# Two unused stretches in the shared SBUF pool: operands of TensorE at multiples of 256 bytes

## The chip, the cores and the metric

The kernel runs on one core of one Trainium2 chip. The metric is the time of one execution on the device in microseconds (us). The figures here come from three timed runs, and from one further execution that the hardware profiler recorded (the trace).

## The reference: what is computed

The program is a small decoder trunk on a sequence of 256 tokens with 1024 channels, in float32. It has two layers, and each layer is a half-step feed-forward block (FFN), a token mixer, and a second half-step FFN. The first layer mixes with Mamba-2, the second with sliding-window attention to a shared K and V. Every sub-layer normalises its input first. Cut to what matters:

```
def swiglu_half_step(h, g, w1, w3, w2):
    u = rmsnorm(h, g)
    return h + FFN_HALF * ((jax.nn.silu(u @ w1) * (u @ w3)) @ w2)

for layer in range(DEPTH):                       # DEPTH = 2
    h = swiglu_half_step(h, ffn_norm[layer, 0], ...)
    if layer < N_A_LAYERS:                       # layer 0
        h = h + mamba2_mixer(rmsnorm(h, ssm_norm[i]), ...)
    else:                                        # layer 1
        h = h + sliding_window_attention(rmsnorm(h, attn_norm[j]), k_shared, v_shared, ...)
    h = swiglu_half_step(h, ffn_norm[layer, 1], ...)
    if layer == N_A_LAYERS - 1:
        k_shared, v_shared = shared_kv(h, kv_norm, w_kv, k_norm)
return h
```

The four FFNs have 1024 x 2816 weights `w1` and `w3` and 2816 x 1024 weights `w2`; they hold most of the arithmetic.

## The kernel before

**Split operands.** TensorE multiplies in float32r. To keep float32 accuracy each operand is split into a high part and a low part, both float32r, and a product is the sum of three matmuls (`mm3` and `wmm3`, lines 135 to 145): high by high, high by low, low by high. All of them are issued by `mm` at line 111, so nearly every matmul of the profile stands under line 108, and one tells them apart by the names of their tiles.

**Weights.** A `Unit` (line 149) loads 1 MB of weights from HBM into `raw` over SP's DMA queue. ScalarE copies it to the high part `wh` (line 171), VectorE subtracts to get the low part `wl` (line 172). There are 8 buffers of each.

**The operands that are not weights.** In a feed-forward block, and in the projections of the mixers, they live in three places:

- `uT`, the normalised input, high and low, 16 KB for each partition in the pool `const` (line 90). `Norm.normalize` (line 294) writes it.
- `vh` and `vl`, the input times the gain but not yet normalised, tag `v` in the pool `sb` (`Norm.open`, line 252, and `Norm.split`, line 256). The first two chunks of each FFN (`c < 2`, line 356), the first gates of Mamba (`z_first`, line 653) and the queries (`q_mm`, line 953) use these, so that TensorE can begin before the statistics of the norm are known. Mamba borrows the same tag for `xdt` (line 676) and the last FFN for `rows` (line 423).
- `ghl`, the gated product of an FFN chunk, high and low halves side by side, tag `ghl` in `sb`, 4 buffers (line 345). Mamba's `yhl` (line 804) shares the tag.

**How an FFN goes.** `run_ffn` (line 306) runs over 11 chunks of 256 hidden columns. For each chunk, `up` multiplies by `w1` and `w3`, `gate` makes `ghl`, and `flush` multiplies the gated product of the chunk before by `w2` into four accumulators (`acc`). From chunk 2 on, `up_wide` (line 370) streams high and low parts of `uT` together, 512 columns at once, and then 256 columns for `wl`. The narrow form streams 256 columns at a time. In the last FFN, `down_t` (line 400) turns the roles round: `ghl` is the stationary operand, and 512 columns of weights stream past it. The queries (`pq`) do the same with `vh` and `vl`.

**Order of the work.** The planner of the tile framework puts the instructions of each engine in order and places the semaphores. It also places tiles: within a pool, tags lie one behind the other in the order in which the code first asks for them, each size rounded up to 32 bytes; a pool opened later lies behind. In the built kernel before the change the start addresses within each partition, with the remainder by 256, are:

| tile | first byte | remainder |
|---|---|---|
| `uT` (pool `const`) | 25,824 | 224 |
| `wh`, first of 8; `wl`, first of 8 | 67,136; 99,904 | 64 |
| tag `g` (first of the pool `sb`) | 132,672 | 64 |
| tag `v`: `vh`, `vl` | 135,744 and 143,936 | 64 |
| `rsb`, `cv` | 152,256; 154,304 | 192 |
| `ghl` / `yhl`, 4 of 2,048 bytes | 158,400 | 192 |
| `sq` | 166,592 | 192 |
| end of `sb`, start of `xp`, `mp`, `ap` | 171,584 | 64 |

Rows of `uT`, `vh`, `vl` and the two halves of `ghl` are 1,024 bytes apart, and the 128 weights that a matmul holds begin 512 bytes apart within `wh` and `wl`. Each of these tensors therefore has one remainder by 256 for all its matmuls.

Of the kernel before, what the change touches and what calls it, by code (L numbers as in the profile page):

```python
# [11 lines left out]
F32 = mybir.dt.float32  # L12
# [6 lines left out]
P = 128  # L19
# [21 lines left out]
def yoco_kernel(ctx: ExitStack, tc: tile.TileContext, a: dict, out: bass.AP):  # L41
# [7 lines left out]
    sb = ctx.enter_context(tc.tile_pool(name="sb", bufs=2))  # L49
# [15 lines left out]
    def x_part(b):  # L65
        nc.sync.dma_start(xin[:, :, b * 256:(b + 1) * 256], xsrc[:, :, b * 256:(b + 1) * 256])

    x_part(0)
    grow = [sb.tile([4 * KT, P], F32, tag="g", name="grow0", bufs=3),
            sb.tile([3 * KT, P], F32, tag="g", name="grow1", bufs=3)]  # L70
    nc.scalar.dma_start(grow[0], a["ffn_norm"].rearrange("l j (k p) -> (l j k) p", p=P))
# [133 lines left out]
    def keep_warm(n):  # L205
        pw = ps_mm.tile([P, P], F32, tag="mm", name=nm("pw"))
        for i in range(n):
            nc.tensor.matmul(pw, dummy, dummy, start=True, stop=True)
# [932 lines left out]

    n0 = norms[0]
    n0.open()
    w13 = a["ffn_w1"][0, 0], a["ffn_w3"][0, 0]
    keep_warm(10)
    ups = {0: [up_unit(*w13, 0, 0, 4, True, {1: lambda: x_part(1), 3: lambda: x_part(2)}),
# [98 lines left out]
```

## Time and profile before

| | |
|---|---|
| median of three runs | 1044.17 us (1042.39, 1044.17, 1044.38) |
| the profiled execution, own time | 1042.34 us |
| its span in the trace | 1040.6 us, 18036 instructions |
| TensorE (PE) busy | 1028.8 us, 99% of the span, 7160 matmuls |
| weight loads (PEld) | 944.6 us, 91% |
| VectorE (DVE) | 735.1 us, 71% |
| ScalarE (ACT) | 602.9 us, 58% |
| HBM read | 184.90 MB, 179 GB/s over the span |
| granted clock of TensorE | 1.00 |

How to read it: matmuls are pipelined, so the record of one (about 280 ns for 256 columns) overlaps the records of the next two or three. The record's length is therefore not the time that a matmul costs. What it costs in a stream is the distance from start to start (the pace), and that is read from the chain of waits, which gives for a piece of the chain its length and its number of matmuls: length divided by number is the pace.

### The profile page before, as it was taken

The numbers are of one execution on the slowest core, as the hardware profiler recorded it, in microseconds if no ns is written. First come the engines' busy times: TensorE is split into PE (matmuls) and PEld (weight loads), VectorE is DVE, ScalarE is ACT, GpSimd is POOL, SyncE is SP. The second block draws the span as 40 slices with busy tenths as digits, with TensorE's granted clock in tenths as the row PEclk, the third lists the DMA queues.
The fourth block names the chain that finished last, engine by engine and source line by source line (L and its number), as shares of the span: only waits on it lengthen the run. The fifth ranks groups of instructions, "written<-read, shape, count | busy, mean of one in ns | idle before, by whom it ended". The sixth has DMA issues, their size and how long they took to land.

```text
span 1040.6 us, 18036 instructions
## 1 busy us (share of the span) xinstructions
PE 1028.8 (99%) x7160; PEld 944.6 (91%) x7160; DVE 735.1 (71%) x1252; ACT 602.9 (58%) x1040; POOL 57.4 (6%) x78
## 2 busy tenths in 40 slices
PE   8899999999999999999999999999999999999998
PEld 8899999999999999999999999999996699888887
DVE  6866656789999988656556975665677678565653
ACT  6564545668976756455545754455567565455551
POOL 1100000003220010000000000100002000000000
PEclk9999999999999999999999999999999999999999
DMA  8676565658564365746465555594641436464641
GB/s 284 172 243 202 165 200 185 180 170 255 166 180 163 124 204 163 234 158 215 163 203 188 177 171 195 174 299 162 217 162 41 123 116 210 162 210 161 221 136 41
DMA packets 139589, 187.19 MB, mean 180 GB/s; under 512 B 5100, under 2 KB 122000, under 8 KB 139504
## 3 DMA queue, kind: packets, MB, share of 16 engines
q1 hardware_dynamic: 137168, 179.32, 52.8%
q0 software_dynamic: 2288, 6.69, 2.4%
q8 instruction: 56, 0.92, 0.4%
q14 instruction: 29, 0.24, 0.1%
q10 hardware_dynamic: 48, 0.02, 0.0%
HBM read 184.90 MB, written 1.11 MB: 179 GB/s over the span
## 4 chain that ended last, share of the span: by engine, by line
PE 91%; DVE 3%; DMA 3%; ACT 1%; SPq 1%; issue 0%; POOL 0%; DVEq 0%; ACTq 0%
PE pm L108 45%; PE acc L108 23%; PE pp L108 9%; PE pa L108 5%; DMA raw<-in_ffn_w_dram 2%; PE pq L106 2%; PE pa L106 1%; PE py L108 1%; DVE wl L172 1%; PE pz L108 1%; PE ps L106 1%; PE po L106 1%; DVE sp L997 1%; SPq L158 1%; PE pkv L108 1%; DMA raw<-in_ssm_w_in_dram 1%
## 5 line engine op out<-in xcount | busy, mean ns | idle before, releaser
L172 DVE TENSOR_TENSOR wl<-raw,wh 128x1024 fp32r<-128x1024 f32 (+1 forms) x372 | 412.2, 1130 | 87.3 <-ACT wh L171 86.9
L171 ACT CAST wh<-raw 128x1024 fp32r<-128x1024 f32 (+1 forms) x372 | 347.5, 970 | 110.5 <-PE acc L108 43.6
L108 PE MATMUL pm<-uT,wh 128*128 128x512 f32 (+1 forms) x1216 | 403.9, 381 | 1.7 <-DVE tp L330 1.6
L108 PE MATMUL pm<-uT,wl 128*128 128x256 f32 x1152 | 321.5, 280 | 0.0
L108 PEld LDWEIGHTS pm<-uT,wh 128*128 128x128 f32 x1216 | 223.6, 188 | 45.3 <-DVE tp L330 2.4
L108 PEld LDWEIGHTS pm<-uT,wl 128*128 128x128 f32 x1152 | 216.6, 188 | 1.0
L108 PE MATMUL acc<-ghl,wh 128*128 128x256 f32 x1056 | 190.6, 281 | 0.6 <-ACT ghl L347 0.6
L339 ACT COPY lo<-pm 128x256 f32<-128x256 f32 x136 | 50.3, 370 | 198.0 <-PE pm L108 198.0
L108 PEld LDWEIGHTS acc<-ghl,wh 128*128 128x128 f32 x1056 | 162.2, 188 | 2.9 <-ACT ghl L347 0.9
L340 DVE TENSOR_TENSOR tp<-pm,lo 128x256 f32<-128x256 f32 x136 | 57.5, 423 | 129.5 <-ACT lo L339 129.4
L108 PE MATMUL acc<-ghl,wl 128*128 128x256 f32 x528 | 148.5, 282 | 0.0
L108 PE MATMUL pp<-uT,wh 128*128 128x256 f32 x576 | 104.8, 283 | 0.1
L108 PEld LDWEIGHTS acc<-ghl,wl 128*128 128x128 f32 x528 | 99.4, 188 | 0.0
L108 PEld LDWEIGHTS pp<-uT,wh 128*128 128x128 f32 x576 | 88.8, 189 | 0.7 <-DVE uT L304 0.3
L108 PE MATMUL pp<-uT,wl 128*128 128x256 f32 x288 | 80.7, 281 | 0.0
L108 PE MATMUL pm<-vh,wh 128*128 128x256 f32 x256 | 73.3, 287 | 1.3 <-ACT wh L171 1.3
L108 PE MATMUL pm<-vh,wl 128*128 128x256 f32 x256 | 72.4, 284 | 0.5 <-DVE wl L172 0.5
L108 PE MATMUL pm<-vl,wh 128*128 128x256 f32 x256 | 72.3, 283 | 0.0
L108 PE MATMUL acc<-wh,ghl 128*128 128x512 f32 x176 | 58.3, 395 | 0.0
L108 PEld LDWEIGHTS pp<-uT,wl 128*128 128x128 f32 x288 | 54.3, 188 | 0.0
L347 ACT CAST ghl<-g 128x256 fp32r<-128x256 f32 x88 | 35.5, 403 | 31.7 <-DVE g L344 31.4
L108 PEld LDWEIGHTS pm<-vh,wh 128*128 128x128 f32 x256 | 48.9, 191 | 1.4 <-ACT wh L171 1.4
(236 smaller groups left out, 1253.5 us busy)
## 6 DMA issues: line engine op xcount, KB each, us to landing
raw<-in_ffn_w_dram SPq DMA_DIRECT2D x168, 512.0 KB, 4.9
raw<-in_ffn_w_dram SPq DMA_DIRECT2D x44, 1024.0 KB, 5.4
raw<-in_ssm_w_in_dram SPq DMA_DIRECT2D x16, 1024.0 KB, 5.5
raw<-in_ssm_w_out_dram SPq DMA_DIRECT2D x8, 1024.0 KB, 5.3
raw<-in_ssm_w_in_dram SPq DMA_DIRECT2D x8, 512.0 KB, 5.1
pr<-pdram POOLq DMA_DIRECT2D x8, 512.0 KB, 4.6
raw<-in_w_q_dram SPq DMA_DIRECT2D x4, 1024.0 KB, 5.0
raw<-in_w_o_dram SPq DMA_DIRECT2D x4, 1024.0 KB, 5.1
```

Source lines behind the costliest of these rows:

```text
L106: r = op(*args, **kw)
L108: r = op(*args, **kw)
L158: nc.sync.dma_start(view(raw, shape, lo, n0)[:, k0:k0 + src.shape[1]], src)
L171: return (nc.scalar.copy(wh, rs).ins, nc.vector.tensor_sub(wl, rs, wh.bitcast(F32)).ins)
L172: nc.vector.tensor_sub(wl, rs, wh.bitcast(F32)).ins)
L339: nc.scalar.copy(lo, pw[:, 256:512])
L340: nc.vector.tensor_add(o, pw[:, 0:256], lo)
L347: nc.scalar.copy(gh, g)
L997: chain[1] = op(*args, **kw).ins
```

## The change

Two tiles that no instruction reads or writes are asked for in the pool `sb`. The first, 48 floats (192 bytes), is asked for ahead of the tag `g`; the second, 32 floats (128 bytes), behind the tag `v`.

```diff
@@ -66,6 +66,7 @@
     x_part(0)
+    sb.tile([P, 48], F32, tag="gap0", name="gap0", bufs=1)
     grow = [sb.tile([4 * KT, P], F32, tag="g", name="grow0", bufs=3),
             sb.tile([3 * KT, P], F32, tag="g", name="grow1", bufs=3)]
@@ -1141,6 +1142,7 @@
     n0 = norms[0]
     n0.open()
+    sb.tile([P, 32], F32, tag="gap1", name="gap1", bufs=1)
     w13 = a["ffn_w1"][0, 0], a["ffn_w3"][0, 0]
```

Added up from the sizes, `g` moves to 132,864 and `v` to 135,936 (both 192 bytes on); `rsb`, `cv`, `ghl` and `sq` move 320 bytes on, to 152,576, 154,624, 158,720 and 166,912. All of these are multiples of 256. What lies behind, the pools `xp`, `mp` and `ap`, moves by 320 bytes too and begins at 171,904 (remainder 128). `uT`, `raw`, `wh` and `wl` stay where they are. No instruction is added, removed or given another size.

## The prediction

> **What bounds the kernel now.** First the page: which engine is busy, and what the chain that ended last is made of.
>
> ```profile
> PE 1028.8 (99%) x7160; PEld 944.6 (91%) x7160; DVE 735.1 (71%) x1252; ACT 602.9 (58%) x1040; POOL 57.4 (6%) x78
> ...
> PEclk9999999999999999999999999999999999999999
> ...
> PE 91%; DVE 3%; DMA 3%; ACT 1%; SPq 1%; issue 0%; POOL 0%; DVEq 0%; ACTq 0%
> PE pm L108 45%; PE acc L108 23%; PE pp L108 9%; PE pa L108 5%; DMA raw<-in_ffn_w_dram 2%; PE pq L106 2%; PE pa L106 1%; PE py L108 1%; DVE wl L172 1%; PE pz L108 1%; PE ps L106 1%; PE po L106 1%; DVE sp L997 1%; SPq L158 1%; PE pkv L108 1%; DMA raw<-in_ssm_w_in_dram 1%
> ```
>
> TensorE is 91% of the chain, at full clock throughout. The only way for a move of tiles to reach the end is therefore the pace of the matmuls. The waits of PE say the same: the longest sums are small.
>
> ```profile
> PE pm L108 <- DVE tp L330: 1.6, 1, 1.6
> PE pm L108 <- ACT wh L171: 1.3, 1, 1.3
> ```
>
> Second, the groups by line and form, which give how many matmuls read a tensor that moves.
>
> ```profile
> L108 PE MATMUL acc<-ghl,wh 128*128 128x256 f32 x1056 | 190.6, 281 | 0.6 <-ACT ghl L347 0.6
> L108 PE MATMUL acc<-ghl,wl 128*128 128x256 f32 x528 | 148.5, 282 | 0.0
> L108 PE MATMUL pm<-vh,wh 128*128 128x256 f32 x256 | 73.3, 287 | 1.3 <-ACT wh L171 1.3
> L108 PE MATMUL pm<-vh,wl 128*128 128x256 f32 x256 | 72.4, 284 | 0.5 <-DVE wl L172 0.5
> L108 PE MATMUL pm<-vl,wh 128*128 128x256 f32 x256 | 72.3, 283 | 0.0
> L108 PE MATMUL acc<-wh,ghl 128*128 128x512 f32 x176 | 58.3, 395 | 0.0
> L108 PE MATMUL acc<-wl,ghl 128*128 128x512 f32 x88 | 34.6, 394 | 0.0
> L108 PE MATMUL pa<-yhl,wh 128*128 128x256 f32 x128 | 23.3, 284 | 0.0
> L108 PE MATMUL pa<-yhl,wl 128*128 128x256 f32 x64 | 18.0, 281 | 0.0
> L106 PE MATMUL pq<-wl,vh 128*128 128x512 f32 x32 | 12.5, 390 | 0.0
> L108 PE MATMUL pz<-vl,wh 128*128 128x256 f32 x32 | 9.0, 283 | 0.0
> ```
>
> So 1056 + 528 + 128 + 64 = 1776 matmuls stream 256 columns of the tag `ghl`. The tag `v` is streamed by 3 x 256 = 768 in the FFNs (192 in each) and by 3 x 32 = 96 in Mamba's first gates. With the roles turned, 176 + 88 = 264 matmuls hold `ghl` and 3 x 32 = 96 hold `v`, while 512 columns of weights stream.
>
> Third, the pace. These are pieces of the chain in order of time: start, length, what, how many.
>
> ```profile
> 282.90 16.38 PE pp L108 x138
> ...
> 388.16 7.20 PE pm L108 x60
> ...
> 398.89 7.18 PE pm L108 x60
> 406.07 2.85 PE acc L108 x24
> 408.93 5.75 PE pm L108 x48
> 414.68 5.70 PE acc L108 x48
> ...
> 759.02 8.54 PE acc L108 x72
> 767.56 9.56 PE pq L106 x42
> 838.59 11.26 PE pa L108 x96
> ...
> 876.29 5.58 PE acc L108 x24
> ```
>
> The `pm` pieces from 388 to 415 us are the first two chunks of an FFN, so they stream `v`. Their pace is 7.20/60 = 120.0, 7.18/60 = 119.7 and 5.75/48 = 119.8 ns. The 256-column `acc` pieces stream `ghl`: 5.70/48 = 118.75, 8.54/72 = 118.6 ns; I use 118.7. The `pa` piece streams `uT`: 11.26/96 = 117.3 ns. So does the `pp` piece, 16.38/138 = 118.7 ns. All have the same 256 columns, the same clock and weights with the same remainder, 64. The pace thus differs by up to 2.4 ns from tensor to tensor, but the one tensor `uT` also has two paces, so the remainder does not settle it alone. Ordered by the remainder of the streamed tensor: 64 gives 119.8, 192 gives 118.7, 224 gives 117.4 or 118.7. Of 512 columns, `pq` (remainder 64 held, 64 streamed) goes at 9.56/42 = 227.6 ns and the last FFN's `acc` (192 held, 64 streamed) at 5.58/24 = 232.5 ns.
>
> **The change, part by part.** It removes and adds no instruction. What it may change is five terms.
>
> *1. The gated products, 192 to 0.* No row has a tensor that TensorE streams at remainder 0. The nearest row, counting round the circle of 256, is `uT`: 224 is 32 bytes away, while 64 is 64 bytes away and 192 also 64. `uT` has two paces; the streams of `ghl` start straight behind a stream of `uT` or `v`, as `pa` follows other matmuls, so I take the faster one, 117.4 ns: 1776 x (117.4 - 118.7) = -2.3 us. The bounds: 120.0 ns, the slowest row, gives 1776 x 1.3 = +2.3 us. On the other side, if the order 119.8, 118.7, 117.4 goes on for another 32 bytes by the step that it last made, one gets 116 ns, and 1776 x -2.7 = -4.8 us.
>
> *2. The inputs not yet normalised, 64 to 0.* Not all of these 864 matmuls count. In the first FFN the chain runs through loads while they stream:
>
> ```profile
> 12.44 5.83 DMA raw<-in_ffn_w_dram
> 18.30 1.14 ACT wh L171 x2
> ...
> 26.05 5.03 DMA raw<-in_ffn_w_dram
> ...
> 31.40 6.95 DMA raw<-in_ffn_w_dram
> ```
>
> Until 38.3 us a faster matmul only waits longer for weights, so its 192 are worth nothing. Of Mamba's first gates the last 12 stand ahead of a piece in which the chain is on ScalarE and VectorE:
>
> ```profile
> 200.25 5.75 PE pz L108 x48
> 206.00 1.41 PE pd L108 x12
> ...
> 210.94 1.32 PE pz L108 x11
> ...
> 212.28 1.06 ACT wh L171
> ```
>
> There remain 576 + 84 = 660. Their streams begin behind a wait or small matmuls of the statistics, as the `pp` streams begin behind transposes, so I take `uT`'s slower pace: 660 x (118.7 - 119.8) = -0.7 us. Bounds: 120.0 gives +0.1 us, 117.4 gives -1.6, and 116 gives -2.5 us.
>
> *3. The roles turned.* Held at remainder 0 while weights at 64 stream, `ghl` has no row either. Between 227.6 and 232.5 ns lies 4.9 ns: at best 264 x -4.9 = -1.3 us. As 232.5 is already the slowest row of this kind, I let the other bound lie as far on the other side, +1.3 us, and take 0, for 0 is 64 bytes from either row. `pq` could lose what separates the two rows, 96 x 4.9 = +0.5 us, or gain as much; I take 0 here too.
>
> *4. ScalarE and VectorE.* They read and write the moved tiles, at these durations:
>
> ```profile
> L347 ACT CAST ghl<-g x88: 395/405/408, 30.3 to 1029.3; 128x256 fp32r<-128x256 f32 x88
> L348 DVE TENSOR_TENSOR ghl<-g,ghl x88: 416/424/427, 30.8 to 1029.7; 128x256 fp32r<-128x256 f32 x88
> ```
>
> I cost this at nothing. What hides it is the flush of the chunk before, 24 matmuls or 2.85 us (the piece at 406.07), against 0.41 + 0.42 us for the two. If that cover were gone, a tenth more on each would be 88 x 0.08 = 7 us; a tenth less would be a gain as large. Nothing in PE's waits above lets either through.
>
> *5. What lies behind the pool.* Mamba's and attention's own tiles move by 320 bytes, and with them the operands of their small float32 matmuls. Those are 1% of the chain each (`py`, `ps`, `po` in the chain by line above), and the rows have no pair to compare; I take 0, with 0.5 us to either side as an estimate: 2% of the 3% of the span that these three make up.
>
> The sum is -2.3 - 0.7 = -3.0 us. The profiled execution took 1042.34 us, of which 1040.6 is span, so it would take 1039.3. That execution is 1.83 us under the median of the runs, 1044.17, and I put the forecast on the scale of the medians: **1041.1 us**. With both tensors at 117.4 the sum is -3.9 (1040.3), with both at 118.7 it is -0.7 (1043.5): this is the forecast's own range.
>
> [...]
>
> **The rivals.**
>
> *The address is not the cause.* The paces may belong to how a stream starts, to its order of weights or to its neighbours, and then nothing moves: 1044.2 us. For it speaks that `uT` at one and the same place runs at 117.3 in one stage and at 118.7 in another, which is also `ghl`'s pace. Against it: no `pm` or `pz` piece that streams `v` goes at 117 or 118.7 ns. Only `pd` does, 1.41/12 = 117.5 ns, and there the weights are others, at other addresses and of 32 columns. [...]
>
> *The rounder the address, the slower.* This is the one on the other side. The tensor with the least even start, 224 (a multiple of 32 alone), is the fastest, and the ones at multiples of 64 are slower; at the same remainder as the weights (`v`, 64 on 64) it is slowest. If a start that is even with respect to some inner unit makes the two reads of TensorE meet more often, multiples of 256 would bring `ghl` to `v`'s 120.0 ns: +2.3 + 0.1 = +2.4 us, 1046.6 us, and up to 1.8 us more with term 3. It decides as soon as the `ghl` pieces reach 119.9 ns, that is 1776 x 1.2 = 2.1 us. Against it: `v` and `ghl` are both multiples of 64 and yet 1.1 ns apart.
>
> *The order goes on.* 64, 192, 224, 256: 116 ns for all, -4.8 - 2.5 = -7.3 us, 1036.9 us. For it speaks the order alone, three points; against it that remainder 256 is 0 and lies between 224 and 64.
>
> **How the numbers follow.** The forecast gets 0.42, the address without effect 0.27, rounder is slower 0.18, the order going on 0.13. About 0.2%, or 2.1 us, is what a measurement of this kernel can tell from no change. Of the forecast's own range, two thirds lie below 1042.1 us, so faster has 0.28 + 0.13 and a little from the spread of the runs, 0.43; slower has 0.17 of the second rival and as little, 0.19; within 0.2% the rest, 0.38. The range reaches from 1036.0, just under the order going on, to 1047.5 us, in the middle of the rounder-is-slower case; the forecast's own is 1040.3 to 1043.5.
>
> **What would show it.** In the chain of the changed kernel, the `acc` piece of 72 matmuls at the end of an FFN should be 72 x 117.4 = 8.45 us long instead of 8.54, the `pm` pieces of 60 should be 7.12 instead of 7.20, and the `pa` piece of 96 should still be 11.26. The records of VectorE and ScalarE named above should keep 424 and 405 ns, and the number and order of instructions should be the same. If the `acc` pieces keep 118.7 ns the address is not the cause. If they reach 120, the rounder is the slower. The prediction is wrong in its basis if the time changes while these paces don't, for then it is a move of another tile, or a changed order of instructions, that counts.

## The result, and the profile after

The changed kernel takes 1035.90 us (median of 4 runs, 1034.33 to 1037.60) against 1044.26 us before (4 runs, 1042.39 to 1044.38). The ratio is 0.9922, with a 95% interval of 0.9910 to 0.9935: 8.4 us or 0.8% faster. The forecast was faster by 3.0 us, to 1041.1 us. The measured median lies 0.1 us under the lower end of the stated range (1036.0 to 1047.5 us) and well outside the forecast's own (1040.3 to 1043.5 us). The profiled execution took 1035.51 us, with a span of 1033.8 us.

The built kernel has the tiles where the change wanted them (`g`, `v` and `ghl` at remainder 0, `uT` at 224, the weights at 64), and each engine issues the same instructions in the same order as before. Only durations and waits can differ.

The page of the kernel after, busy times and the chain that ended last:

```profile
PE 1020.2 (99%) x7160; PEld 934.7 (90%) x7160; DVE 734.6 (71%) x1252; ACT 602.9 (58%) x1040; POOL 57.1 (6%) x78
...
PE 82%; issue 6%; DVE 6%; DMA 3%; ACT 1%; SPq 1%; POOL 0%; POOLq 0%; DVEq 0%; ACTq 0%
```

TensorE is busy for 8.6 us less (1028.8 before), its weight loads, 7160 like the matmuls, for 9.9 us less (944.6 before), and no other engine's busy time changed by as much as a microsecond. TensorE's share of the chain fell from 91% to 82%. Of the 6% of "issue", 53 us are one piece at 799 us behind which the chain could not be followed; but DVE rose from 3% to 6%, and that is real: with faster matmuls there are stretches, at the starts of the sub-layers, where VectorE's work now ends last: the low parts of weights and of `v`, and the norm statistics behind them (`wl` is 2% of the chain, 1% before; `vl` and `sq` are 1% each).

The pace stands in the chain of waits of the kernel after (start, length, what, how many):

```profile
282.84 16.19 PE pp L109 x138
...
327.77 16.37 PE pp L109 x138
...
398.02 6.82 PE pm L109 x60
...
413.00 5.44 PE acc L109 x48
...
424.01 2.73 PE acc L109 x24
...
581.62 7.07 PE pm L109 x60
...
591.52 5.65 PE pm L109 x48
597.17 5.65 PE acc L109 x48
...
753.25 8.18 PE acc L109 x72
761.43 9.61 PE pq L107 x42
...
869.80 5.49 PE acc L109 x24
```

`v` went from 120.0 ns to 6.82/60 = 113.7 in one FFN and to 7.07/60 = 117.8 in another; `ghl` from 118.7 to 5.44/48 = 113.3 and 8.18/72 = 113.6, and 5.65/48 = 117.7 at 597 us. Most pieces of `ghl` are those between two pieces of the wide form; there it goes at 2.73/24 = 113.8. The two paces come with the same tiles at the same addresses. In two places one pace goes with a whole stretch: from 581 to 603 us the pieces, `v` and `ghl` by turns, go at 117.7 and 117.8, and from 398 to 418 us the same ones at 113.3 to 113.7. `uT` did not move, and its `pp` piece is now at its other known pace (16.19/138 = 117.3 instead of 118.7), while the one at 327 us keeps 118.6.

Both traces hold the same 7160 matmuls in the same order, so one can subtract, matmul by matmul, the distance from one start to the next. The last matmul starts 7.15 us earlier. Differences under 60 ns (the pace) sum to -11.6 us: -7.4 for `ghl` in the accumulators, -0.7 for `yhl`, -3.7 for `v` (of which -0.5 in Mamba's first gates), -0.5 for the last FFN with the roles turned, and +0.7 for the rest. Larger differences (waits and clock) give back +4.5 us. About 1.6 of these are in the norm statistics: the matmuls around 206, 397, 577 and 854 us wait 0.2 to 0.5 us longer, behind VectorE or, at 397 and 854 us, behind GpSimd. About 2.1 lie at 39 to 46 us, in the first FFN. The waits of PE in the kernel after show both:

```profile
PE pm L109 <- DVE tp L331: 2.3, 1, 2.3
...
PE pc L109 <- DVE sq L272: 0.7, 2, 0.4
```

The first was 1.6 us, the second was not there. And after the first, the clock drops. Here are two stretches of the first FFN, first after, then before, then of `e_ghl0`, a kernel of the experiments below: length, busy time of PE, PEld, DVE, ACT and POOL with their instructions, the granted clock, the share of the DMA engines, GB/s.

```profile
38.80:43.40 4.60, 1.64 (x6) 0.58 (x4) 3.35 (x6) 4.11 (x10) 0.00 (x0) 0.97 0.00 0
43.40:46.90 3.50, 3.45 (x17) 3.45 (x18) 3.50 (x8) 0.72 (x3) 0.00 (x0) 0.55 0.30 62
```

```profile
38.80:43.40 4.60, 2.35 (x12) 1.29 (x11) 3.57 (x7) 4.11 (x10) 0.00 (x0) 1.00 0.00 0
43.40:46.90 3.50, 3.50 (x28) 3.39 (x29) 3.50 (x8) 0.51 (x2) 0.00 (x0) 1.00 0.42 83
```

```profile
38.80:43.40 4.60, 2.48 (x13) 1.43 (x13) 3.64 (x7) 4.11 (x10) 0.00 (x0) 1.00 0.00 0
43.40:46.90 3.50, 3.50 (x20) 3.50 (x20) 3.50 (x8) 0.44 (x2) 0.00 (x0) 0.60 0.42 97
```

After the change TensorE arrives 0.55 us sooner at 39 us (38.82 instead of 39.37), is idle for 2.96 us of the first stretch instead of 2.25, and then runs 3.4 us at half clock (the granted clock is 0.50 in every half microsecond from 43.5 to 46.5 us, and 0.03 x 4.60 x 2 + 0.45 x 3.50 x 2 = 3.4): 17 matmuls in 3.5 us instead of 28. The longer wait is not shown to be the reason: in `e_ghl0` TensorE is idle for 2.12 us, less than before the change, and the clock drops all the same, to a mean of 0.60 over the second stretch. Nor is the drop peculiar to the change. On the chip with most of the later runs of the kernel before, 5 of 25 have a mean clock of 1.000 and a median of 1042.33 us, and 14 have 0.998 and 1043.36 us. The profile of before had 1.000, and the runs of after have 0.997 or 0.998. That can be a part of why the two profiled executions are only 6.8 us apart and the medians 8.4; the clocks of the first runs of before are not on record.

### The profile page after: what moved, and what is told of

Read it like the earlier page. It is cut to its first block, busy times and chain, and to the rows that moved or that the text cites. A ratio compares the mean times of both kernels' runs of the same rounds, so it can differ in the third digit from the quotient of the medians.

```text
span 1033.8 us, 18036 instructions
## 1 busy us (share of the span) xinstructions
PE 1020.2 (99%) x7160; PEld 934.7 (90%) x7160; DVE 734.6 (71%) x1252; ACT 602.9 (58%) x1040; POOL 57.1 (6%) x78
## 4 chain that ended last, share of the span: by engine, by line
PE 82%; issue 6%; DVE 6%; DMA 3%; ACT 1%; SPq 1%; POOL 0%; POOLq 0%; DVEq 0%; ACTq 0%
PE pm L109 43%; PE acc L109 21%; PE pp L109 9%; PE pa L109 3%; DVE wl L173 2%; DMA raw<-in_ffn_w_dram 2%; PE pq L107 2%; PE py L109 1%; DVE vl L259 1%; DVE hT L276 1%; PE ps L107 1%; ACT wh L172 1%; SPq L159 1%; DVE sq L270 1%; PE pkv L109 1%
## 5 line engine op out<-in xcount | busy, mean ns | idle before, releaser
L109 PE MATMUL acc<-ghl,wh 128*128 128x256 f32 x1056 | 185.0, 278 | 0.6 <-ACT ghl L348 0.6
L109 PE MATMUL acc<-ghl,wl 128*128 128x256 f32 x528 | 146.3, 277 | 0.0
L349 DVE TENSOR_TENSOR ghl<-g,ghl 128x256 fp32r<-128x256 f32 x88 | 37.0, 423 | 17.6 <-ACT ghl L348 17.5
```

Source lines behind the costliest of these rows:

```text
L109: r = op(*args, **kw)
L349: nc.vector.tensor_sub(gl, g, gh.bitcast(F32))
```

## The experiments

Three theories stand behind the expectations. **A**: the remainder by 256 of the streamed tensor alone sets its pace, and 0 is a good one. **B**: the difference counts, that is the remainder by 256 of the start of the streamed tensor minus the start of the held weights. After the change it is 0 - 64, or 192, for `v` and `ghl`; before it was 0 for `v`, 128 for `ghl` and 160 for `uT`. **C**: neither; the tiles behind the pool, or the way a stream starts, make the time. All layouts below keep the instructions and their order.

### One tensor at a time

`e_ghl0` moves `ghl` alone to 0, `v` stays at 64:

```diff
     n0.open()
+    sb.tile([P, 16], F32, tag="gap1", name="gap1", bufs=1)
```

> Only the gated products move: one unused stretch of 64 bytes behind the tag v puts ghl at remainder 0, v stays at 64, uT at 224, the weights at 64. Theory A (the pace belongs to the remainder of the tensor that streams): ghl at 113.4 ns as in the changed kernel, v at 119.8 as before; 1776 x 5.3 ns = 9.4 us less in paces, of which a part goes into waits, so about 1037 us. Theory B (the pace belongs to the remainder of the streamed tensor less that of the held weights) expects the same here. Theory C (it is the tiles behind the pool, or the entry into a stream, that counts): ghl keeps 118.7 ns and the time stays near 1044 us.

`e_v0` moves `v` alone to 0; `ghl` lands 256 bytes further on, at remainder 192 as before:

```diff
     x_part(0)
+    sb.tile([P, 48], F32, tag="gap0", name="gap0", bufs=1)
...
     n0.open()
+    sb.tile([P, 16], F32, tag="gap1", name="gap1", bufs=1)
```

> Only the inputs not yet normalised move: 192 bytes ahead of the tag g and 64 behind v put v at 0 and leave ghl at 192. Theories A and B: v at 113.5 or 117.8 ns, ghl at 118.7; 660 matmuls on the path x 4 to 6 ns is 2.5 to 4 us, less what the waits for the norm take back (about 1 us), so 1041 to 1042.5 us. Theory C: v keeps 119.8 ns, about 1044 us.

Measured: `e_ghl0` 1035.95 us (ratio 0.9933, 0.9919 to 0.9948, against 1042.95 us for the kernel before, median of 25 runs on that chip); `e_v0` 1041.05 us (0.9984, 0.9974 to 0.9993). The chain of `e_ghl0` and then of `e_v0`, the same FFN in both:

```profile
398.03 7.18 PE pm L108 x60
...
413.69 5.46 PE acc L108 x48
```

```profile
398.59 6.82 PE pm L109 x60
...
413.91 5.70 PE acc L109 x48
```

Each tensor changes its own pace and leaves the other's: `ghl` 113.8 with `v` still at 119.7 ns, then `v` 113.7 with `ghl` still at 118.8. The gains, 7.0 and 1.9 us, add up to 8.9, close to the 8.4 us of the whole change. So the cause lies in the tiles' places, tensor by tensor, and the larger part of the gain is `ghl`'s. The move of the pools behind, 64 bytes in `e_ghl0` and 320 in the changed kernel, makes no difference that shows. C is out, save for which of two paces a stream takes.

### The remainder itself, or the difference to the weights

`e_abs` puts `uT`, `v` and `ghl` all at remainder 0, but the weights at 96. The difference is 160 for all three, `uT`'s of before. `e_rel` puts all three at 224 and the weights at 32: a difference of 192, `v`'s and `ghl`'s of after.

```diff
     x_part(0)                       # e_abs
+    sb.tile([P, 40], F32, tag="gap0", name="gap0", bufs=1)
...
+    const.tile([P, 8], F32, name="gapu")      # ahead of uT
...
     n0.open()
+    sb.tile([P, 32], F32, tag="gap1", name="gap1", bufs=1)
```

```diff
     x_part(0)                       # e_rel
+    sb.tile([P, 48], F32, tag="gap0", name="gap0", bufs=1)
...
-                self.rsk = const.tile([P, NT], F32, name=nm("rsk"))
+                self.rsk = (sb.tile([P, NT], F32, tag="rsk", name=nm("rsk"), bufs=1) if self.gi
+                            else const.tile([P, NT], F32, name=nm("rsk")))
...
     n0.open()
+    sb.tile([P, 32], F32, tag="gap1", name="gap1", bufs=1)
```

> uT, v and ghl all at remainder 0, the weights at 96 (32 bytes ahead of uT in the pool const move uT and all behind it, the two stretches are cut to fit). The streamed tensors are thus at 0, and the difference streamed less held is 160 for all three, which is uT's difference in the kernel before. Theory A: uT too goes to 113.4 ns in its narrow form, 1376 matmuls x 5 ns = 7 us less than the changed kernel, about 1029 us. Theory B: all three go at uT's paces of before, 117.4 to 118.7 ns, so v and ghl lose their gain: 1040 to 1043 us.

> The weights at 32 (one small tile of 32 bytes goes from const to sb, so raw, wh and wl begin 32 bytes earlier), v and ghl at 224, uT stays at 224: the difference streamed less held is 192 for all three, as it is for v and ghl in the changed kernel, but no streamed tensor is at 0. Theory B: v, ghl and narrow uT all at 113.4 ns or 117.8, about 1029 us. Theory A: all three at 117.4 to 118.7 ns as uT at 224 before, 1040 to 1043 us.

Measured on the same chip: `e_abs` 1040.58 us (0.9977, 0.9968 to 0.9986), as B expected, and `e_rel` 1043.68 us (1.0009, 0.9999 to 1.0018), 15 us above the 1029 that was expected under B. The chain of `e_abs`, then of `e_rel`; `pm` x60 streams `v`, `acc` streams `ghl`, `pa` streams `uT`, and `pm` x32 is 16 pairs of the wide form of `uT`:

```profile
388.72 7.12 PE pm L110 x60
...
414.82 5.63 PE acc L110 x48
...
428.82 5.56 PE pm L110 x32
...
837.39 11.39 PE pa L110 x96
```

```profile
399.17 6.81 PE pm L109 x60
...
414.14 5.44 PE acc L109 x48
...
425.23 2.83 PE acc L109 x24
...
428.05 5.65 PE pm L109 x32
...
839.49 11.31 PE pa L109 x96
```

The wide form of `uT` in the kernel before, for comparison:

```profile
420.38 5.55 PE pm L108 x32
```

At remainder 0, with the difference of `uT` before, `v` and `ghl` get `uT`'s paces: 118.7, 117.3, and `uT` itself, now at 0, keeps 118.6. At remainder 224, with the difference of after, `v` and `ghl` get 113.5 and 113.3 in these pieces, and `uT` 117.8. A says the opposite of both and falls; B stands for which paces a tensor can take.

The time of `e_rel` shows that this is not the whole account, for two reasons. First, the wide form of `uT` rises from 5.55/16 = 347 (and 347.5 in `e_abs`) to 5.65/16 = 353.1 ns for a pair, and there are 1088 pairs: +6.6 us. Second, `ghl` takes the slower of its two paces nearly everywhere: 48 of the 50 pieces of 24 that the chain shows between 50 us and the last FFN go at 2.83/24 = 117.9 ns, where the changed kernel has 113.8 with the same difference of 192. Taken start by start against the kernel before, `ghl` in the accumulators gains 2.5 us here and 7.4 in the changed kernel. All in all the narrow streams gained about 12 us, the wide pairs lost 7 (together -4.9), and 6.3 us came back in waits, one of them in Mamba's mixer (1.2 us for VectorE's `xdt`, 0.2 before). So the layout that is best for `v` and `ghl` is not good for `uT`, most of whose time is in the wide form, and the change under study gains in part because `uT` keeps its difference of 160. The pace of `ghl` depends on more than its own difference; what else decides is not shown.

### A map of the difference

Four layouts move `uT` by adding some of 256 bytes ahead of it and the rest behind it, so that the weights stay at 64, and set `v` and `ghl` with the two gaps in the pool. As an example the first of them, and the numbers of the others:

```diff
+    sb.tile([P, 16], F32, tag="gap0", name="gap0", bufs=1)    # m_uT64: 24; m_uT128, m_uT192: none
+    const.tile([P, 16], F32, name="gapu")                     # ahead of uT: 24, 40, 56
+    const.tile([P, 48], F32, name="gapw")                     # behind uT: 40, 24, 8
+    sb.tile([P, 8], F32, tag="gap1", name="gap1", bufs=1)     # 16, 16, 16
```

> A look at paces. 256 bytes are added to the pool const, 64 of them ahead of uT; weights stay at remainder 64, uT at 32, v at 128, ghl at 32. Differences streamed less held, by 256: uT 224, v 64, ghl 224. Theory B (the difference sets the pace): narrow uT and ghl must show the same pace, whatever it is, and v another; by the order 160 (117.4), 192 (113.4) it could be 109 ns or back towards the 119.8 of difference 0. The pair of 512 and 256 columns, 346.7 ns at 160 and 353.3 at 192, should be slower still, near 360 ns, if it goes on. Theory A (remainder of the streamed tensor alone) has no reason for uT and ghl at 32 to differ either, but none for the pair to follow the difference. Time by the pair alone: 1088 x 13 ns = 14 us more than with uT at 160, so 1035 to 1058 us.

> A look at paces: uT at 64 (difference 0), v at 160 (difference 96), ghl at 96 (difference 32), weights at 64. Theory B: narrow uT now goes at v's pace of the kernel before, 119.8 to 120.0 ns, because the difference is 0; for 32 and 96 there is no row. The pair of 512 and 256 columns is unknown; the queries, 512 columns at difference 0, had 227 ns and 256 columns have 120, which would make 347 ns. Theory A: the same here for uT, as 64 was v's remainder. About 1040 to 1050 us.

> A look at paces: uT at 128 (difference 64), v at 64 (difference 0), ghl at 0 (difference 192). Theory B: ghl 113.4, v 119.8 ns as in the run with ghl alone moved; narrow uT at the pace that v showed at difference 64; the pair of 512 and 256 columns unknown. The last FFN streams 512 columns at difference 64 with 229 ns; with a narrow matmul of 113 to 120 ns the pair would be 342 to 349. About 1030 to 1040 us.

> A look at paces: uT at 192 (difference 128), v at 64 (difference 0), ghl at 0 (difference 192). Theory B: narrow uT at 118.7 ns, which was ghl's pace at difference 128 before; ghl 113.4, v 119.8. The pair: 512 columns at difference 128 went at 232.5 ns in the last FFN before, so 232.5 + 118.7 = 351 ns, 1088 x 4.5 = 5 us more than the run with ghl alone moved, about 1041 us.

One run each, beside 1043.45 us for the kernel before: `m_uT32` 1044.65, `m_uT64` 1046.58, `m_uT128` 1045.34 and `m_uT192` 1041.88 us. No one of them helps, and with single runs differences under 2 us tell nothing; they were made for the paces. `m_uT128` missed its expectation of 1030 to 1040 us: the wide pair went at 353 ns and not at 342 to 349, `ghl` took the slower pace in 25 of 50 pieces of 24, and at 327 us its chain has a slow stretch, 30 matmuls of `pp` at 5.17/30 = 172.3 ns with 113 at 113.4 behind them (mean clock of that run 0.997). The chains of `m_uT32`, `m_uT64`, `m_uT128` and `m_uT192`, in this order:

```profile
389.73 7.07 PE pm L111 x60
...
400.28 6.81 PE pm L111 x60
...
415.58 5.68 PE acc L111 x48
...
840.86 11.36 PE pa L111 x96
```

```profile
390.58 7.20 PE pm L111 x60
...
417.08 5.65 PE acc L111 x48
...
841.17 11.52 PE pa L111 x96
```

```profile
423.04 5.66 PE pm L110 x32
...
840.69 11.31 PE pa L110 x96
```

```profile
420.95 5.62 PE pm L110 x32
...
837.44 11.40 PE pa L110 x96
```

Two last layouts move only the weights (with 128 or 64 bytes behind `uT`) and keep `uT` at 224. They also ask whether a layout is better than the changed one, for `v` and `ghl` are kept at difference 192 while `uT` gets 32 or 96:

```diff
+    sb.tile([P, 48], F32, tag="gap0", name="gap0", bufs=1)
+    const.tile([P, 32], F32, name="gapw")                     # behind uT; b_uT96: 16
+    sb.tile([P, 32], F32, tag="gap1", name="gap1", bufs=1)
```

> A version that might beat both, and the missing point of the map. 128 bytes are added to const behind uT, so weights are at 192 and uT stays at 224 (difference 32); v and ghl at 128 (difference 192, as in the changed kernel). Theory B: v and ghl at 113.4 or 117.8 ns though no remainder of a streamed tensor is one that had that pace before; narrow uT at ghl's pace at difference 32, 117.5 to 118.0. The pair of 512 and 256 columns has not been seen at 32: at 346.7 ns, its lowest so far, the time is the changed kernel's, 1036 us; at 353 it is 7 us more; if it is lower, it beats both kernels. Theory A: v and ghl at 128 have no row, narrow uT at 224 stays at 117.4 to 118.7.

> The same with 64 bytes behind uT: weights at 128, uT at 224 (difference 96), v and ghl at 64 (difference 192). Theory B: v, which at remainder 64 went at 119.8 ns in the kernel before, now goes at 113.4 or 117.8, and ghl too; narrow uT at 119.9, v's pace at difference 96. Theory A: v at 64 goes at 119.8 as before. The pair of 512 and 256 columns at 96 has not been seen; with narrow uT slower by 1 to 2 ns x 1376, 1038 us if the pair stays at 346.7.

Measured against 1043.69 us for the kernel before: `b_uT32` 1037.33 us (0.9946, 0.9931 to 0.9960), `b_uT96` 1039.70 us (0.9962, 0.9949 to 0.9975). The chain of `b_uT32`, then of `b_uT96`:

```profile
328.17 16.10 PE pp L110 x138
...
398.07 7.07 PE pm L110 x60
...
424.82 2.83 PE acc L110 x24
```

```profile
400.14 6.82 PE pm L110 x60
...
420.56 5.61 PE pm L110 x32
...
836.46 11.52 PE pa L110 x96
```

Neither beats the changed kernel, which took 1033.69 us on this chip (`a_again`, below). In `b_uT32` the wide pair stays at 347 ns and the narrow form of `uT` gains, but `ghl` goes at 2.83/24 = 117.9 ns in 49 of 50 such pieces, as in `e_rel`. Start by start that costs 4.4 us against `a_again`.

In `b_uT96` `v` stands at remainder 64 again, where it ran at 120.0 ns before the change, and runs at 6.82/60 = 113.7: only the weights are elsewhere (128). That is the plainest single case for B. All paces by the difference, worked out as length by number from pieces of these chains, quoted ones and others like them (16 wide pairs are a piece of 32; a piece of 24 gives its pace to about 0.4 ns):

| difference | 256 columns, ns | read from | wide pair of `uT`, ns |
|---|---|---|---|
| 0 | 119.7 to 120.0 | `v` before and in `e_ghl0`, `uT` in `m_uT64` | 347, some 353 |
| 32 | 116.7 to 118 | `uT` in `b_uT32`, `ghl` in `m_uT64` | 347 |
| 64 | 113.5 or 117.8 | `v` in `m_uT32`, `uT` in `m_uT128` | 352.5 to 353.8 |
| 96 | 120.0 | `v` in `m_uT64`, `uT` in `b_uT96` | 350.6, some 352.5 |
| 128 | 118.3 to 120 | `ghl` before and in `e_v0`, `uT` in `m_uT192` | 351.2 |
| 160 | 117.1 to 120 | `uT` before, after and in `a_again`, all in `e_abs` | 347 to 348 |
| 192 | 113.3 to 114.6, or 117.5 to 117.9 | `v` and `ghl` after, all in `e_rel`, `v` in `b_uT96`, `ghl` in `m_uT192` and `b_uT32` | 353.1 |
| 224 | 118.3 | `uT` and `ghl` in `m_uT32` | 347, some 353 |

In every row the tensors named agree, and in four rows (32, 96, 160, 192) they agree although their own remainders differ. In the other four the tensors are different ones at the same remainder. The narrow form is fastest at 64 and 192, where the wide pair is slowest. Two things speak for 256 as the period. Taken by 512, the differences in the changed kernel are 192 for `v` and 448 for `ghl`, and both have the same two paces. And 128 would be too short, for the wide pair mostly goes at 347 ns at 0 and at 351 at 128.

### The changed kernel again, and without the drop of the clock

`a_again` is the changed kernel as it is, on the chip of `b_uT32` and `b_uT96`. `b_warm` adds to it five small products with a tile of zeros (ten entries in the trace, 1.28 us), added to an accumulator in the wait at 39 us, to keep TensorE busy. They add zero.

```diff
                         while pend:
+                            if pre and len(pend) == 1:
+                                for _ in range(5):
+                                    with tc.issue_after(pe[-1]):
+                                        nc.tensor.matmul(acc[0][:, 0:P], dummy, dummy, start=False, stop=False)
                             flush(pend.pop(0))
```

> The changed kernel once more, with a new trace. Theory B (the difference streamed less held sets which paces a stream can take; where there are two, the way in which a stream starts decides): every ghl and v piece at 113.4 or 117.8 ns, nothing between, though the same piece may take the other of the two in this execution; 1034 to 1038 us. If the two paces belonged to a place in the program, the same pieces would be at 117.8 as in the first trace (the v pieces that end near 589, 861 us and the ghl piece that ends near 603 us).

> The changed kernel with five matmuls of zeros by zeros added to an accumulator (they add 0) in the wait near 39 us, where the changed kernel's TensorE sat idle for 2.3 us and then ran at half clock for 3.4 us. If that wait brings the clock down, and five times 0.22 us of work is enough to keep it up, the mean granted clock is 1.000 and the 24 matmuls behind the wait go at 113 instead of 213 ns, 1.5 to 2 us less than the changed kernel: about 1034 us. If the clock falls in any case, or did in the kernel before as well, the time is that of the changed kernel or up to 0.3 us more.

Measured: `a_again` 1033.69 us (0.9912, 0.9897 to 0.9927), `b_warm` 1032.92 us (0.9901, 0.9884 to 0.9917). The first is the change's gain a second time, 10.0 us against the 1043.69 us of the kernel before on this chip. `b_warm`'s interval overlaps it, so its 0.8 us less are not told apart from none. The clock did stay up, in the trace and, at 0.999 to 1.000, in all its four runs. The same windows as above, of `b_warm`:

```profile
38.80:43.40 4.60, 4.09 (x29) 3.38 (x29) 4.60 (x10) 2.69 (x7) 3.33 (x9) 1.00 0.06 15
43.40:46.90 3.50, 3.50 (x22) 2.73 (x21) 3.50 (x6) 0.00 (x0) 1.79 (x3) 1.00 0.91 297
```

But the edit did more than that: GpSimd works in both windows where it had stood still, and other work lies around the wait, for the planner, given five more matmuls, placed its instructions otherwise. In the profiled executions `b_warm` is 2.3 us ahead of `a_again` at the FFN near 396 us and 2.0 us at the end (spans of 1031.9 and 1033.9 us). A part goes where it fell into the slower one of the two paces. The chain of `b_warm` and of `a_again`:

```profile
395.90 7.07 PE pm L109 x60
```

```profile
327.77 16.56 PE pp L109 x138
...
398.18 6.82 PE pm L109 x60
```

So what the half clock alone costs the changed kernel was not isolated; for the kernel before, the two groups of runs above differ by 1.0 us. Of the four runs of `a_again`, the one with clock 1.000 took 1033.83 us and the other three, at 0.997 to 0.998, 1033.29 to 1035.63, so no cost of the drop shows there. `a_again` also shows how far the two paces repeat. The FFNs at 398 and 581 us have the same paces as in the first trace of this kernel, 113.7 and 117.8, but `pp` at 327.77 us takes 16.56 us (120.0 ns) where it took 16.37 us (118.6) at the same time of that trace. Which of its paces a stretch takes is therefore not settled by the addresses alone.

## Why the prediction was right in sign and too small in size

**Term 1, the gated products: right sign, mis-sized.** The step that failed is "the nearest row, counting round the circle of 256, is `uT`", from which 117.4 ns and -2.3 us came. Measured are 113.3 to 113.8 ns for most streams of `ghl`, and -8.1 us for `ghl` and `yhl` together. Nearness of remainders is not what counts. `uT` stood at 224 with difference 160, and the new place has difference 192, of which the trace of before had no row. `e_abs` makes the step's own case, `uT`'s difference, and gets the forecast's figures: paces of 117.3 and 118.7, and a median 2.4 us below before, where the step promised about 3. The bound of -4.8 us, a step of 32 bytes further, failed too: three rows that were ordered by the wrong quantity cannot bound a fourth.

**Term 2, the inputs not yet normalised: same failure.** 118.7 ns was taken, 113.4 to 117.8 came; -0.7 us was forecast, and -3.7 us is measured for all 864 matmuls. That the first FFN's 192 matmuls of `v` would be worth nothing held. TensorE comes to its wait at 39 us 0.55 us sooner, waits 0.76 us longer there, and restarts its accumulators at 43.45 instead of 43.24 us. Of Mamba's first gates the prediction counted 84 of 96, and that was too many. TensorE is 0.45 us ahead of the kernel before when the first of them begins at 200 us, and 0.28 us at 216 us, behind the last: it waits 0.5 us longer for VectorE at 207 us, between them. The gates' gain of 0.5 us went into that wait.

**Term 3, the roles turned:** 0 with 1.3 us to either side was forecast. The `acc` piece of 24 is 5.49 instead of 5.58 us long, and all 264 together gave -0.5 us; `pq` takes 9.61 instead of 9.56 us for 42, which is +0.1 us for 96. Inside the bounds.

**Term 4, ScalarE and VectorE: held.** The rows of the moved tile after the change:

```profile
L348 ACT CAST ghl<-g x88: 394/406/410, 30.4 to 1022.3; 128x256 fp32r<-128x256 f32 x88
L349 DVE TENSOR_TENSOR ghl<-g,ghl x88: 414/424/427, 30.9 to 1022.7; 128x256 fp32r<-128x256 f32 x88
```

They were 405 and 424 ns. At this layout the move shows in the pace of TensorE and not in the durations of the other two engines that touch the tile.

**Term 5, what lies behind the pool: held, as far as the medians tell.** `e_ghl0` and the changed kernel move those pools by 64 and 320 bytes; their gains are 7.0 and 8.4 us, and `v` alone brings 1.9.

**What the sum left out.** It took the whole gain of a pace to the end, apart from the places that it named. Of -11.6 us of pace, 4.5 came back: 1.6 at norm statistics, where VectorE or GpSimd now ends last, and about 2.1 in the first FFN, with the half clock. The second is in the difference of the two profiles more than in that of the medians, if the runs of before had the drop as most of its later runs did (mean clock under 1.000 in 20 of 25). The 1.83 us by which I raised the forecast to the scale of the medians may have that cause in part; this is not shown.

**The rivals.** That the address is not the cause fell with `e_ghl0` and `e_v0`. That rounder is slower fell with the 113.4 ns of the changed kernel; but its remark that a tensor at the weights' own remainder is slowest holds, in the row for difference 0 (119.7 to 120.0 ns), with the row for 96 as slow (120.0). That two reads of TensorE meet, as it supposed, was a guess that no run shows. The order going on came nearest in time, 1036.9 against 1035.9 us, and for no good reason: it had the remainder of the streamed tensor as its quantity, which `e_abs` refutes (remainder 0 at 117.3 and 118.7 ns), and one pace of 116 ns for all, where `ghl` and `v` have two, near 113.5 and 117.8.

**What was in the trace already.** The prediction says of `v` that it stands on 64 with weights on 64. One look at the three tensors by their difference (0, 128, 160) would have said that the new one, 192, was unexplored; that calls for bounds to both sides wide of the rows, and not for the nearest row.

## What to carry to other kernels

Where a kernel is TensorE's pace throughout, the start of the streamed tensor relative to the held weights is worth a few runs: for 256 columns of float32r it made 113.3 to 120.0 ns, 6%, for 192 or 128 bytes of padding that no instruction touches. Set it for each tensor and each form apart (here 192 gave the narrow form its fastest pace, 113.3 ns, and the wide pair one of its slowest, 353.1), and read it from pieces of the chain, length by number, since the records of single matmuls overlap (278 ns on average for `ghl` in the changed kernel, at a pace of 113.8). Measure the layout as a whole, for `ghl` at one and the same difference went at 113.8 or 117.9 ns when `uT` or the weights stood elsewhere. And expect part of a faster pace back wherever another engine was just in time: here 1.6 of 11.6 us came back at the norm statistics.

## What the runs showed of the hardware that was not expected

- In these layouts the pace of a float32r matmul at full clock went with the difference by 256 of its two operands' starts: 113.3 to 120.0 ns for 256 columns, and 347 to 353.8 ns for a pair of 512 and 256, and not in the same order. Why is not shown.
- At one and the same layout two paces occur, such as 113.4 and 117.8 ns at 64 and at 192. In the changed kernel one pace held across changes of the streamed tensor from 398 to 418 us (113.3 to 113.7) and from 581 to 603 us (117.7 and 117.8), while `v` went at 117.8 at 854 us and at 5.46/48 = 113.8 at 864 us, with a piece of the turned roles between. In two traces of the changed kernel some stretches agree (113.7 and 117.8 ns at 398 and 581 us) and some don't (`pp` at 327.77 us, 118.6 and 120.0). The layout of the other tensors has a part in it: between pieces of the wide form `ghl`, at 192 each time, goes at 113.8 ns in the changed kernel and at 117.9 in `e_rel` and `b_uT32`. What chooses between the two stays open.
- Half clock came for 3.4 us after 2.96 us of idle time within 4.60 us in the changed kernel (granted clock 0.55 from 43.40 to 46.90 us), and it came after 2.12 us in `e_ghl0` (0.60), but not after 2.25 us in the kernel before (1.00). The sum of the idle time alone therefore does not decide it. TensorE's longest single gap there was 2.33 us in the changed kernel and 1.57 us in the kernel before, and behind each came two matmuls that took 1.09 us together. What brings the clock down is not shown.
